# Row norms by halves of the columns, and part of the first block's softmax moved from VectorE to ScalarE, in a three-block transformer kernel

## The chip, the cores and the metric

The kernel runs on one core of one Trainium2 chip, as one launch. The metric is the device time of one execution in microseconds; lower is better. Engines are named as in the profile: PE is TensorE (PEld its weight loads), DVE is VectorE, ACT is ScalarE, POOL is GpSimd, SP is SyncE, which issues nearly all the DMAs.

## The reference, cut to what matters

Three transformer blocks are applied one after the other to one sequence of 256 rows of 1024 columns, all in fp32. Each block begins with a modulated RMS norm of the rows, and each ends with an RMS norm with a gain. In the first block the attention's softmax has one more logit per head, the sink:

```python
def rmsnorm(x, g):
    xf = x.astype(jnp.float32)
    y = xf * lax.rsqrt(jnp.mean(xf * xf, axis=-1, keepdims=True) + NORM_EPS)
    return (y * g.astype(jnp.float32)).astype(x.dtype)

# hybrid_layer, the first block
hx = modulate(rmsnorm(x, norm1_g), sh1x, sc1x)
hc = modulate(rmsnorm(ctx, norm1_g), sh1c, sc1c)
...
# windowed_attention: 16 heads, 256 own and 256 context keys
probs = jax.nn.softmax(jnp.concatenate([s_loc, s_ctx, sink_b], axis=-1), axis=-1)
p_loc = probs[..., :n_loc].astype(vn.dtype)
...
h2x = modulate(rmsnorm(x, norm2_g), sh2x, sc2x).reshape(B * L, D)
y = moe_ffn(h2x, w_router, b_router, w_gu, b_gu, w_down, b_down)
x = x + g2x * y.reshape(B, L, D)
```

## The kernel before

Rows lie on the 128 partitions, so the 256 rows are two tiles a = 0, 1 of 128 rows and 1024 columns. The stages run in this order, with their times in the profiled execution: the first block's projections, windowed attention, pooling and gates (0 to 318 us), its mixture of experts (318 to 1285), the second block's mixer (1285 to 1563), its peer layer (1563 to 2432), and the third block (2432 to the end at 2756). The expert weights stream through SP's DMA queue, and a loop at the end of that stage is a barrier for all engines.

Every fp32 weight tile is cut into two parts before PE uses it: ACT rounds it (`wh`, L151) and DVE subtracts (`wl`, L152); three matmuls per tile follow (L169, L194, L1707). Each of these helpers works tile by tile just ahead of PE, so a late `wl` or `wh` is a wait of PE.

The order on each engine is not the order of the code: a list scheduler places every instruction when the program is built, from its dependencies. A change of one stage therefore moves instructions of other work that lies beside it.

Norms: `rms_stats` (L310) takes for a = 0 the sum of squares on ACT (L318) and for a = 1 on DVE (L320), adds the constant on DVE (L321) and raises to the power -1/2 on POOL (L322). `scaled` (L325) multiplies the rows by it, a = 0 on DVE (L328) and a = 1 on ACT (L329). It is used by the first block for x and for the context, before the experts, and before the peer layer. `normed` (L332) joins the norm that ends a block with the norm that begins the next one (second and third block): two sums of squares per tile, L345 on ACT and L349 or L351, the product with the gain (L346), the power on POOL (L354) and the scaled rows (L355). `finish` (L358) later writes the rows of the residual stream. PE's transposes (L373) of the scaled rows follow, and `hl_T` writes their high and low parts (L414 to L422).

Attention of the first block: 16 turns (8 pairs of heads, two tiles of rows). `scores` makes for each of the two heads i the score matmuls on PE (L631, L632), bias and row minimum on DVE (L633, from PSUM), the exponentials on ACT (L635, with their sum), and the sink's share: a subtraction on DVE (L636) and a small exponential on ACT (L637). Then, one turn later, the sum and reciprocal on DVE (L647, L648), the normalization of both heads on DVE (L650, 128x512 each), the transposes on PE (L653) and the copies out of PSUM on ACT (L657) and DVE (L659). The modulation's weight sums (`ada_group`: ACT L291, DVE L292, POOL or DVE L294) are laid between the turns. Experts: the router's matmul is L832, its logits L834, its exponentials L845 on ACT, and the mask and ranks L850 to L880 on DVE.

Of the kernel before, what the change touches and what calls it, by code (L numbers as in the profile page):

```python
# [16 lines left out]
P = 128  # L17
# [4 lines left out]
D = 1024  # L22
# [6 lines left out]
def bcast_rows(ap1d, n=P):  # L29

    return ap1d.unsqueeze(0).broadcast_to([n, ap1d.shape[-1]])
# [28 lines left out]
def body(tc, A, out, stages=("b1", "moe", "b2", "peer", "b3"), dbg=None):  # L60
# [31 lines left out]
    with Pool("cst") as cst, Pool("ring", bufs=RING) as ring, Pool("psum", nb={"ps": 4, "pd": 3, "pa": 1}, space=PSUM) as psp:  # L92
# [217 lines left out]
        def rms_stats(pool, src, n, eps, tag="rs"):  # L310

            m = len(src)
            r = pool(tag + "_r", [P, m], bufs=2)
            for i, s in enumerate(src):
# [17 lines left out]
        def normed(pool, eps, tag, at_once=False):  # L332
# [6 lines left out]
            v = pool("nv", [P, 4])  # L339
            w = pool("nw", [P, 2])  # L340

            for a in range(2):
                v2, wa = v[:, 2 + a : 3 + a], w[:, a : a + 1]
                j = pool("b4", [P, D])
                nc.scalar.activation(j, x[:, a, :], AF.Square, accum_out=v[:, a : a + 1])  # L345
                nc.vector.tensor_tensor(xg[:, a, :], x[:, a, :], gb, ALU.mult)  # L346
                j = pool("b4", [P, D])
                if a == 0 and at_once:
                    nc.vector.tensor_tensor_reduce(j, xg[:, a, :], xg[:, a, :], 1.0, 0.0, ALU.mult, ALU.add, v2)  # L349
                else:  # L350
                    sq = nc.scalar.activation(j, xg[:, a, :], AF.Square, accum_out=v2)  # L351
                nc.vector.tensor_scalar(v2, v2, 1.0 / D, eps * eps1, ALU.mult, ALU.add)
                nc.vector.scalar_tensor_tensor(wa, v[:, a : a + 1], eps / D, v2, ALU.mult, ALU.add)
                nc.gpsimd.tensor_tensor(wa, wa, mhalf[:, 0:1], ALU.pow)  # L354
                ins = nc.vector.tensor_scalar(xs[:, a, :], xg[:, a, :], wa, None, ALU.mult)  # L355
            K.normed_by = (sq.ins, ins.ins)

            def finish():  # L358
                with K.tc.issue_after(K.parts_made.ins):
                    nc.vector.tensor_scalar(v[:, 0:2], v[:, 0:2], 1.0 / D, eps1, ALU.mult, ALU.add)  # L360
                nc.gpsimd.tensor_tensor(v[:, 0:2], v[:, 0:2], mhalf[:, 0:2], ALU.pow)
                nc.vector.tensor_scalar(x[:, 0, :], xg[:, 0, :], v[:, 0:1], None, ALU.mult)
                nc.scalar.activation(x[:, 1, :], xg[:, 1, :], AF.Copy, scale=v[:, 1:2])
# [164 lines left out]
def block1(K):  # L528
# [3 lines left out]
    with Pool("b1", nb=nb) as wp:  # L532
# [36 lines left out]
        nc.sync.dma_start(nsink, bcast_rows(A["attn_sink"]))  # L569
        nc.vector.tensor_scalar(nsink, nsink, -1.0, None, ALU.mult)  # L570
# [1549 lines left out]
```

## Time and profile before

| what | value |
|---|---|
| time, median of 3 runs | 2755.48 us (2755.38 to 2757.06) |
| the profiled execution | 2757.8 us |
| its span, first to last instruction | 2755.9 us |
| mean granted clock of TensorE | 0.974 of full speed |
| PE busy | 2572.7 us, 93% |
| DVE, ACT, POOL busy | 1532.8, 1022.6, 210.2 us |

The profiled execution lies 0.08% above the median, and 1.9 us of its time lie around its span. PE is the engine that is busy nearly always, so what matters is where PE waits, and for whom. An engine's busy share over the whole span says little: in the first block's attention DVE is at nine tenths in each slice of the page, in the experts' stage at one or two.

### The profile page before, as it was taken

To read this page: it belongs to the slowest core of one execution; us is meant where nothing else is said; L and a number is where in the kernel's file an instruction comes from. 1 tells how busy PE (TensorE), PEld (TensorE's weight loads), DVE (VectorE), ACT (ScalarE), POOL (GpSimd) and SP (SyncE) were. 2 spreads that over 40 slices of the span, in tenths; PEclk is the share of its full clock that TensorE was granted. 3 is DMA by queue.
4 is the path that set the end of the run, shared out by engine and by line. 5 is a ranking of instruction groups with operands and counts; after the bars stand their busy time and mean duration, and the time that the engine had idled before them with its cause. 6 is when DMAs were issued, how large, how long until landed. Compare 5 with 4: busy or idle time off the path is not lost. (4 is left out here: it accounts for less than half of the span.)

```text
span 2755.9 us, 36667 instructions
## 1 busy us (share of the span) xinstructions
PE 2572.7 (93%) x14235; PEld 1773.2 (64%) x14235; DVE 1532.8 (56%) x2574; ACT 1022.6 (37%) x1611; POOL 210.2 (8%) x125
## 2 busy tenths in 40 slices
PE   7999998999799979997999999999999999989998
PEld 4767742333233313333766798999888888878897
DVE  4997621122112201114787799687777675567777
ACT  3665300010001000002554443886555444455554
POOL 1221000000000000001112013100111000010000
PEclk9999999999999999999999999999999999999999
DMA  7668699999999999998565444679787785554452
GB/s 288 231 226 324 254 399 414 424 421 394 413 424 424 408 424 424 424 424 321 171 205 212 148 156 151 204 225 322 275 311 281 249 296 197 188 192 138 167 185 77
DMA packets 154017, 786.02 MB, mean 285 GB/s; under 512 B 14961, under 2 KB 49649, under 8 KB 70001
## 3 DMA queue, kind: packets, MB, share of 16 engines
q1 hardware_dynamic: 153840, 783.66, 75.0%
q8 instruction: 113, 1.85, 0.3%
q14 instruction: 64, 0.52, 0.0%
HBM read 765.78 MB, written 17.83 MB: 284 GB/s over the span
## 5 line engine op out<-in xcount | busy, mean ns | idle before, releaser
L152 DVE TENSOR_TENSOR wl<-w,wh 128x1024 fp32r<-128x1024 f32 x361 | 456.1, 1269 | 169.8 <-ACT wh L151 160.1
L151 ACT CAST wh<-w 128x1024 fp32r<-128x1024 f32 x379 | 393.1, 1042 | 341.1 <-PE pd L169 97.6
L169 PE MATMUL pd<-wh,b 128*128 128x512 f32 (+1 forms) x944 | 262.0, 395 | 1.1 <-POOL b L419 0.5
L936 PE MATMUL pd<-w,xd 128*64 128x512 f32 (+2 forms) x864 | 243.6, 606 | 3.9 <-DMA w<-in_w_gu 3.9
L169 PEld LDWEIGHTS pd<-wh,b 128*128 128x128 f32 x944 | 173.7, 189 | 46.4 <-issue 8.8
L1707 PE MATMUL pd<-wh,b 128*128 128x512 f32 x630 | 194.6, 390 | 1.3 <-DVE b L1692 0.7
L902 DVE TENSOR_SCALAR b<-pd 128x512 f32<-128x512 f32 x28 | 19.4, 691 | 254.1 <-PE pd L937 254.1
L169 PE MATMUL pd<-wl,b 128*128 128x512 f32 (+1 forms) x472 | 149.9, 396 | 5.9 <-DVE wl L152 5.9
L936 PEld LDWEIGHTS pd<-w,xd 128*64 128x64 f32 (+2 forms) x864 | 70.9, 133 | 114.2 <-issue 101.5
L955 DVE TENSOR_TENSOR b<-pd,g 128x512 f32<-128x512 f32 x28 | 19.3, 690 | 215.7 <-PE pd L937 215.7
L936 PE MATMUL pd<-wB,xd 128*64 128x512 f32 (+2 forms) x392 | 133.6, 601 | 4.9 <-DMA wB<-in_w_gu 4.9
L901 ACT ACTIVATE b<-b 128x512 f32<-128x512 f32 x28 | 17.7, 631 | 309.6 <-DVE b L900 309.6
L1707 PEld LDWEIGHTS pd<-wh,b 128*128 128x128 f32 x630 | 115.9, 188 | 24.0 <-DVE b L1692 1.1
L936 PE MATMUL pd<-w,at 128*64 128x512 f32 (+2 forms) x384 | 117.2, 667 | 13.1 <-DMA w<-in_w_down 12.5
L936 PE MATMUL pd<-wA,xd 128*64 128x512 f32 (+2 forms) x272 | 113.6, 646 | 4.8 <-DMA wA<-in_w_gu 4.8
L893 ACT ACTIVATE xd<-ps,mod,gs 128x128 f32<-128x128 f32 x56 | 25.2, 457 | 241.0 <-PE ps L889 162.4
L900 DVE TENSOR_SCALAR b<-pd 128x512 f32<-128x512 f32 x28 | 19.3, 690 | 165.0 <-PE pd L937 165.0
L1707 PE MATMUL pd<-wl,b 128*128 128x512 f32 x315 | 105.5, 389 | 0.0
L169 PEld LDWEIGHTS pd<-wl,b 128*128 128x128 f32 x472 | 87.3, 189 | 28.0 <-DVE wl L152 8.4
L1669 PE MATMUL ps<-b,wh 128*128 128x256 f32 x384 | 96.2, 292 | 2.8 <-ACT wh L151 2.8
L1575 DVE TENSOR_TENSOR b<-iota,slt 128x512 f32<-128x512 f32 x128 | 84.9, 711 | 21.1 <-PE pd L1583 21.1
L152 DVE TENSOR_TENSOR xT<-w,xT 128x1024 fp32r<-128x1024 f32 x53 | 67.1, 1266 | 50.6 <-ACT xT L151 50.6
(638 smaller groups left out, 5662.3 us busy)
## 6 DMA issues: line engine op xcount, KB each, us to landing
w<-in_w_gu SPq DMA_DIRECT2D x108, 1024.0 KB, 19.1
w<-in_peer_u SPq DMA_DIRECT2D x64, 1024.0 KB, 5.1
w<-in_peer_v SPq DMA_DIRECT2D x64, 1024.0 KB, 5.1
w<-in_w_down SPq DMA_DIRECT2D x59, 1024.0 KB, 19.5
w<-in_w_in SPq DMA_DIRECT2D x50, 1024.0 KB, 5.3
wB<-in_w_gu SPq DMA_DIRECT2D x49, 1024.0 KB, 19.6
w<-in_w_ada SPq DMA_DIRECT2D x48, 1024.0 KB, 6.4
wA<-in_w_gu SPq DMA_DIRECT2D x34, 1024.0 KB, 19.5
```

What stands on the lines that cost most here:

```text
L151: nc.scalar.copy(h, raw)
L152: (eng or nc.vector).tensor_tensor(l, raw, h.bitcast(F32), ALU.subtract)
L169: ins = mm(o, h[:, kk - k0 + k, a * P : (a + 1) * P], w[:, k * n : (k + 1) * n], start=(kk == k0 and m == 0 and k == 0), stop=(kk == k0 + ...
L893: nc.scalar.activation(d, s, AF.Identity, bias=sh[:, q : q + 1], scale=gs[:, q : q + 1])
L900: nc.vector.tensor_scalar(g, psg, 7.0, None, ALU.min)
L901: nc.scalar.activation(s, g, AF.Tanh, scale=0.851)
L902: nc.vector.tensor_scalar(l, psl, 7.0, -7.0, ALU.min, ALU.max)
L936: mm(ps[r], xt[:, k, r], ws[i][k // 4][:, k % 4, :], start=(k == 0), stop=False, skip_group_check=True)
L955: nc.vector.tensor_tensor(y, ps, g2[:, c * 512 : (c + 1) * 512], ALU.mult)
L1575: nc.vector.tensor_tensor(o, iota.unsqueeze(1).broadcast_to([P, 4, P]), SLT[:, v, t0 : t0 + 4].unsqueeze(2).broadcast_to([P, 4, P]), ALU.i ...
L1669: mm(o, wh[:, c], hh[:, k, :], start=(k == 0), stop=False)
L1707: ins = mm(acc[2 * a + c], p[:, i, a * P : (a + 1) * P], q[:, c * 512 : (c + 1) * 512], start=(first and i == 0 and n == 0), stop=(last an ...
```

## The change

Three edits are made. First, in `rms_stats` for rows of 1024 columns, and in `normed`, every square and every product with the gain is made for the left and the right 512 columns apart, with small additions that join the two sums; the scratch tiles come from the ring `b2` in place of `b4`. In `normed` the loop over the halves is the outer one and the loop over the tiles the inner one. Second, in `scores` the subtraction on DVE and the exponential over two columns are replaced by two exponentials over one column on ACT, with the sink as their bias; a copy of the sink row with its sign kept is made once on ACT. Third, the normalization of the second head of each turn (i = 1) is made on ACT with a scale in place of DVE.

```diff
@@ -311,6 +311,23 @@
 
             m = len(src)
             r = pool(tag + "_r", [P, m], bufs=2)
+            if n == D:
+
+                vs = [pool(tag + "_h", [P, 3], bufs=3) for _ in src]
+                for h in range(2):
+                    for i, s in enumerate(src):
+                        v, sh = vs[i], s[:, h * 512 : (h + 1) * 512]
+                        j = pool("b2", [P, 512])
+                        if i % 2 == 0:
+                            nc.scalar.activation(j, sh, AF.Square, accum_out=v[:, h : h + 1])
+                        else:
+                            nc.vector.tensor_tensor_reduce(j, sh, sh, 1.0, 0.0, ALU.mult, ALU.add, v[:, h : h + 1])
+                        if h == 0:
+                            nc.vector.tensor_scalar(v[:, 0:1], v[:, 0:1], n * eps, None, ALU.add)
+                        else:
+                            nc.vector.tensor_scalar(v[:, 2:3], v[:, 1:2], v[:, 0:1], 1.0 / n, ALU.add, ALU.mult)
+                            nc.gpsimd.tensor_tensor(r[:, i : i + 1], v[:, 2:3], mhalf[:, 0:1], ALU.pow)
+                return r
             for i, s in enumerate(src):
                 j = pool("b4", [P, n])
                 v = pool(tag + "_v", [P, 2], bufs=3)
@@ -336,31 +353,38 @@
             gb, eps1 = K.pending
             K.pending = None
             xg, xs = [pool(tag, [P, 2, D]) for _ in range(2)]
-            v = pool("nv", [P, 4])
-            w = pool("nw", [P, 2])
-
-            for a in range(2):
-                v2, wa = v[:, 2 + a : 3 + a], w[:, a : a + 1]
-                j = pool("b4", [P, D])
-                nc.scalar.activation(j, x[:, a, :], AF.Square, accum_out=v[:, a : a + 1])
-                nc.vector.tensor_tensor(xg[:, a, :], x[:, a, :], gb, ALU.mult)
-                j = pool("b4", [P, D])
-                if a == 0 and at_once:
-                    nc.vector.tensor_tensor_reduce(j, xg[:, a, :], xg[:, a, :], 1.0, 0.0, ALU.mult, ALU.add, v2)
-                else:
-                    sq = nc.scalar.activation(j, xg[:, a, :], AF.Square, accum_out=v2)
-                nc.vector.tensor_scalar(v2, v2, 1.0 / D, eps * eps1, ALU.mult, ALU.add)
-                nc.vector.scalar_tensor_tensor(wa, v[:, a : a + 1], eps / D, v2, ALU.mult, ALU.add)
-                nc.gpsimd.tensor_tensor(wa, wa, mhalf[:, 0:1], ALU.pow)
-                ins = nc.vector.tensor_scalar(xs[:, a, :], xg[:, a, :], wa, None, ALU.mult)
+            v = pool("nv", [P, 2, 2, 2])
+            w = pool("nw", [P, 2, 2])
+
+            for h in range(2):
+                c = slice(h * 512, (h + 1) * 512)
+                for a in range(2):
+                    va, wa = v[:, a], w[:, a, :]
+                    j = pool("b2", [P, 512])
+                    nc.scalar.activation(j, x[:, a, c], AF.Square, accum_out=va[:, 0, h : h + 1])
+                    nc.vector.tensor_tensor(xg[:, a, c], x[:, a, c], gb[:, c], ALU.mult)
+                    j = pool("b2", [P, 512])
+                    if a == 0 and h == 1 and at_once:
+                        nc.vector.tensor_tensor_reduce(j, xg[:, a, c], xg[:, a, c], 1.0, 0.0, ALU.mult, ALU.add, va[:, 1, h : h + 1])
+                    else:
+                        sq = nc.scalar.activation(j, xg[:, a, c], AF.Square, accum_out=va[:, 1, h : h + 1])
+                    if h == 0:
+                        nc.vector.tensor_scalar(wa[:, 1:2], va[:, 0, 0:1], eps, D * eps * eps1, ALU.mult, ALU.add)
+                        nc.vector.tensor_tensor(wa[:, 1:2], wa[:, 1:2], va[:, 1, 0:1], ALU.add)
+                        continue
+                    nc.vector.scalar_tensor_tensor(wa[:, 0:1], va[:, 0, 1:2], eps, va[:, 1, 1:2], ALU.mult, ALU.add)
+                    nc.vector.tensor_scalar(wa[:, 0:1], wa[:, 0:1], wa[:, 1:2], 1.0 / D, ALU.add, ALU.mult)
+                    nc.gpsimd.tensor_tensor(wa[:, 0:1], wa[:, 0:1], mhalf[:, 0:1], ALU.pow)
+                    ins = nc.vector.tensor_scalar(xs[:, a, :], xg[:, a, :], wa[:, 0:1], None, ALU.mult)
             K.normed_by = (sq.ins, ins.ins)
 
             def finish():
                 with K.tc.issue_after(K.parts_made.ins):
-                    nc.vector.tensor_scalar(v[:, 0:2], v[:, 0:2], 1.0 / D, eps1, ALU.mult, ALU.add)
-                nc.gpsimd.tensor_tensor(v[:, 0:2], v[:, 0:2], mhalf[:, 0:2], ALU.pow)
-                nc.vector.tensor_scalar(x[:, 0, :], xg[:, 0, :], v[:, 0:1], None, ALU.mult)
-                nc.scalar.activation(x[:, 1, :], xg[:, 1, :], AF.Copy, scale=v[:, 1:2])
+                    nc.vector.tensor_tensor(v[:, :, 0, 0], v[:, :, 0, 0], v[:, :, 0, 1], ALU.add)
+                    nc.vector.tensor_scalar(w[:, :, 1], v[:, :, 0, 0], 1.0 / D, eps1, ALU.mult, ALU.add)
+                nc.gpsimd.tensor_tensor(w[:, :, 1], w[:, :, 1], mhalf[:, 0:2], ALU.pow)
+                nc.vector.tensor_scalar(x[:, 0, :], xg[:, 0, :], w[:, 0, 1:2], None, ALU.mult)
+                nc.scalar.activation(x[:, 1, :], xg[:, 1, :], AF.Copy, scale=w[:, 1, 1:2])
 
             return xs, finish
 
@@ -567,6 +591,8 @@
         nc.gpsimd.memset(band[:, :, T : 2 * T], 0.0)
         nc.sync.dma_start(band[:, :, 0:T], A["c_band"])
         nc.sync.dma_start(nsink, bcast_rows(A["attn_sink"]))
+        sink = wp("sink", [P, 16])
+        nc.scalar.copy(sink, nsink)
         nc.vector.tensor_scalar(nsink, nsink, -1.0, None, ALU.mult)
 
         def bias(c):
@@ -633,8 +659,9 @@
                 nc.vector.tensor_tensor_reduce(p[:, i, :], ps, band[:, a, :], -1.0, nsink[:, h : h + 1], ALU.add, ALU.min, ng[:, i : i + 1])
             for i in range(2):
                 nc.scalar.activation(p[:, i, :], p[:, i, :], AF.Exp, scale=-1.0, bias=ng[:, i : i + 1], accum_out=es[:, 2 + i : 3 + i])
-            nc.vector.tensor_tensor(es[:, 0:2], ng, nsink[:, 2 * hp : 2 * hp + 2], ALU.subtract)
-            nc.scalar.activation(es[:, 0:2], es[:, 0:2], AF.Exp)
+            for i in range(2):
+                h = 2 * hp + i
+                nc.scalar.activation(es[:, i : i + 1], ng[:, i : i + 1], AF.Exp, bias=sink[:, h : h + 1])
             return p, es
 
         turns = [(hp, a) for hp in range(8) for a in range(2)]
@@ -647,7 +674,10 @@
             nc.vector.tensor_tensor(rs, es[:, 0:2], es[:, 2:4], ALU.add)
             nc.vector.reciprocal(rs, rs)
             for i in range(2):
-                nc.vector.tensor_scalar(p[:, i, :], p[:, i, :], rs[:, i : i + 1], None, ALU.mult)
+                if i == 0:
+                    nc.vector.tensor_scalar(p[:, i, :], p[:, i, :], rs[:, i : i + 1], None, ALU.mult)
+                else:
+                    nc.scalar.activation(p[:, i, :], p[:, i, :], AF.Copy, scale=rs[:, i : i + 1])
                 pt = pst()
                 for s in range(4):
                     nc.tensor.transpose(pt[:, s * P : (s + 1) * P], p[:, i, s * P : (s + 1) * P], ident)
```

In the whole program ACT has 1575 instructions in place of 1530 and DVE 2470 in place of 2472; PE, POOL and SP have the same numbers of instructions.

**DVE in a turn of the attention.** The tiles `b_269`, `b_280` are exponentials of two heads, `es` their sums, `rs` the reciprocals; L697 belongs to the pooling. Before:

```order
L668 TENSOR_TENSOR b_148_732<-pa_1216,b_147_731 128x256
L636 TENSOR_TENSOR es_1236<-ng_1235,nsink_111 128x2
L648 RECIPROCAL rs_287_1251<-rs_287_1251 128x2
L697 SCALAR_TENSOR_TENSOR b_385_1681<-pd_1706,cols_66,b_384_1680 128x256
L650 TENSOR_SCALAR b_269_1184<-b_269_1184,rs_287_1251 128x512 x2
L647 TENSOR_TENSOR rs_297_1290<-es_1236 128x2
L697 SCALAR_TENSOR_TENSOR b_385_1681<-pd_1715,cols_66,b_384_1680 128x256
L648 RECIPROCAL rs_297_1290<-rs_297_1290 128x2
L697 SCALAR_TENSOR_TENSOR b_385_1681<-pd_1724,cols_66,b_384_1680 128x256
L659 COPY b_286_1250<-ps_1262 128x4x128
L292 SCALAR_TENSOR_TENSOR aw_1180<-aw_1181,cpad_84,aw_1180 128x1024
```

And of the changed kernel, a turn further on (L674, L675 and L678 are the former L647, L648 and L650, L727 the former L697):

```order
L659 ISA b_297_1289,ng_1290<-ps_1296,band_116,nsink_117 128x512
L659 ISA ng_1290 128x1
L674 TENSOR_TENSOR rs_302_1304<-es_1250 128x2
L727 SCALAR_TENSOR_TENSOR b_390_1695<-pd_1720,cols_66,b_389_1694 128x256
L675 RECIPROCAL rs_302_1304<-rs_302_1304 128x2
L727 SCALAR_TENSOR_TENSOR b_390_1695<-pd_1729,cols_66,b_389_1694 128x256
L678 TENSOR_SCALAR b_285_1248<-b_285_1248,rs_302_1304 128x512
L292 SCALAR_TENSOR_TENSOR aw_1244<-aw_1245,cpad_84,aw_1244 128x1024
L674 TENSOR_TENSOR rs_318_1366<-es_1291 128x2
```

The subtraction into `es` is gone, and one multiplication stands where there were two. On ACT of the changed kernel the same turn reads as follows (L661 is the former L635, L664 the new sink exponential, L680 the new normalization, L687 the former L657):

```order
L726 ACTIVATE b_389_1694<-pd_1729,cols_66 128x256
L291 ACTIVATE aw_1244<-aw_1244,cpad_84 128x1024
L726 ACTIVATE b_389_1694<-pd_1738,cols_66 128x256
L661 ACTIVATE b_297_1289,es_1291<-b_297_1289,ng_1290 128x512
L664 ACTIVATE es_1291<-ng_1290,sink_455 128x1
L661 ACTIVATE b_297_1289,es_1291<-b_297_1289,ng_1290 128x512
L664 ACTIVATE es_1291<-ng_1290,sink_455 128x1
L680 ACTIVATE b_285_1248<-b_285_1248,rs_302_1304 128x512
L687 COPY b_290_1263<-ps_1308 128x4x128
```

The normalization of the tile `b_285` has come to stand behind the four exponentials of the next turn's tile `b_297`.

**ACT at the start of the experts' stage.** L318 is the sum of squares of tile 0, L393 the modulated transposes, L329 the scaled rows of tile 1, L845 the router's exponentials. Before:

```order
L318 ACTIVATE b_591_2690,rs_v_2691<-x_68 128x1024
L393 ACTIVATE wF_2623<-ps_2661,gs_2659 128x256
L393 ACTIVATE wF_2623<-ps_2668,gs_2659 128x256
L393 ACTIVATE wF_2623<-ps_2675,gs_2659 128x256
L393 ACTIVATE wF_2623<-ps_2682,gs_2659 128x256
L329 ACTIVATE b_578_2644<-x_68,rs_r_2689 128x1024
L845 ACTIVATE ex_2723,sm_2724<-tv_2715,ng_2721 128x4
L845 ACTIVATE ex_2752,sm_2753<-tv_2744,ng_2750 128x4
```

And of the changed kernel (L322, L417, L346 and L875 are the same steps):

```order
L322 ACTIVATE b_598_2706,rs_h_2704<-x_68 128x512
L417 ACTIVATE wF_2637<-ps_2675,gs_2673 128x256
L417 ACTIVATE wF_2637<-ps_2682,gs_2673 128x256
L417 ACTIVATE wF_2637<-ps_2689,gs_2673 128x256
L417 ACTIVATE wF_2637<-ps_2696,gs_2673 128x256
L322 ACTIVATE b_600_2712,rs_h_2704<-x_68 128x512
L346 ACTIVATE b_583_2658<-x_68,rs_r_2703 128x1024
L875 ACTIVATE ex_2743,sm_2744<-tv_2735,ng_2741 128x4
L875 ACTIVATE ex_2772,sm_2773<-tv_2764,ng_2770 128x4
```

The second half of the squares has come to stand behind the four modulated transposes.

**DVE in the second block's projections.** L152 makes the `wl` tiles, L1339 to L1341 (L1369 to L1371 in the changed kernel) a softmax over the forget-gate bounds with a 128x512 reciprocal, L1213 copies compressed keys out of PSUM. Before:

```order
L523 TENSOR_TENSOR b_1532_7175<-b_1560_7339,b_1561_7340 128x256 x2
L152 TENSOR_TENSOR wl_7386<-w_7349,wh_7385 128x1024
L152 TENSOR_TENSOR wl_7402<-w_7349,wh_7401 128x1024
L1339 TENSOR_TENSOR h_1699_7974<-lb_7442,lb_7443 128x512
L1340 RECIPROCAL h_1699_7974<-h_1699_7974 128x512
L511 TENSOR_TENSOR b_1574_7419<-b_1530_7173,rt_7096 128x512
L1341 TENSOR_TENSOR lb_7442<-lb_7442,h_1699_7974 128x512
L525 TENSOR_TENSOR b_1531_7174<-b_1574_7419,b_1575_7420 128x512
L511 TENSOR_TENSOR b_1576_7425<-b_1530_7173,rt_7096 128x512
L1213 COPY b_1599_7473<-ps_7474 64x255
L525 TENSOR_TENSOR b_1531_7174<-b_1576_7425,b_1577_7426 128x512
L1213 COPY b_1599_7473<-ps_7474 64x255
```

And of the changed kernel (L1195, L1197 and L1200 copy projections out of PSUM, L535 belongs to the rotation):

```order
L1369 TENSOR_TENSOR h_1710_8009<-lb_7477,lb_7478 128x512
L1197 COPY vs_7212<-pd_7214 128x128
L152 TENSOR_TENSOR wl_7311<-w_7288,wh_7310 128x560
L1195 COPY b_1544_7211<-pd_7215 128x256
L1370 RECIPROCAL h_1710_8009<-h_1710_8009 128x512
L1197 COPY vs_7212<-pd_7215 128x128
L152 TENSOR_TENSOR wl_7327<-w_7290,wh_7326 128x560
L152 TENSOR_TENSOR wl_7343<-w_7290,wh_7342 128x560
L1371 TENSOR_TENSOR lb_7477<-lb_7477,h_1710_8009 128x512
L152 TENSOR_TENSOR wl_7389<-w_7382,wh_7388 128x1024
L1200 COPY vs_7212<-pd_7292 128x128
L535 TENSOR_TENSOR b_1569_7366<-b_1541_7208,rt_7116 128x384
```

The reciprocal has moved up in front of the last two `wl` tiles of the 560-column projection; before, it stood behind all of these and ahead of the L1213 copies.

## Rows read from the trace of the kernel before

**Rows 1.** The page's busy times.

```profile
PE 2572.7 (93%) x14235; PEld 1773.2 (64%) x14235; DVE 1532.8 (56%) x2574; ACT 1022.6 (37%) x1611; POOL 210.2 (8%) x125
```

**Rows 2.** Stretches: length, busy us of five engines, granted clock, DMA; sum over 90 to 240.

```profile
110.00:120.00 10.00, 10.00 (x56) 7.87 (x55) 8.93 (x21) 5.80 (x15) 0.00 (x0) 0.89 0.78 261
...
sum 150.00, PE 137.82 PEld 100.13 DVE 133.03 ACT 90.08 POOL 26.75; mean PE 9.19 PEld 6.68 DVE 8.87 ACT 6.01 POOL 1.78
```

**Rows 3.** What PE waited for, 94 to 210: total, times, longest.

```profile
PE ps L653 <- DVE b L650: 4.6, 4, 2.7
...
PE ps L653 <- DVE es L636: 2.2, 1, 2.2
```

**Rows 4.** DVE groups, 94 to 206: busy us, mean ns, idle before.

```profile
L650 DVE TENSOR_SCALAR b<-b,rs 128x512 f32<-128x512 f32 x32 | 15.3, 512 | 0.2
...
L636 DVE TENSOR_TENSOR es<-ng,nsink 128x2 f32<-128x2 f32 x16 | 6.4, 401 | 0.0
```

**Rows 5.** Groups on ACT, 94 to 206.

```profile
L635 ACT ACTIVATE b<-b,ng 128x512 f32<-128x512 f32 x32 | 22.9, 716 | 7.4 <-DVE ng L633 7.3
...
L657 ACT COPY b<-ps 128x512 f32<-128x512 f32 x16 | 9.3, 579 | 9.7 <-PE ps L653 9.6
...
L637 ACT ACTIVATE es<-es 128x2 f32<-128x2 f32 x16 | 3.1, 194 | 2.5 <-DVE es L636 2.5
```

**Rows 6.** Timeline, 168 to 178.5: start, duration, instruction, [PE's idle time, who ended it].

```profile
168.63 2.35 POOL L294 TENSOR_TENSOR aacc<-aacc,aw 128x1024 f32<-128x1024 f32 x1 [18.94 <-DVE aw L292]
168.71 2.28 DVE L636 TENSOR_TENSOR es<-ng,nsink 128x2 f32<-128x2 f32 x1
...
171.38 0.87 DVE L650 TENSOR_SCALAR b<-b,rs 128x512 f32<-128x512 f32 x2
...
172.00 1.06 PE L653 MATMUL ps<-ident,b 128*128 128x128 f32 x8 [2.70 <-DVE b L650]
...
175.13 2.36 POOL L294 TENSOR_TENSOR aacc<-aacc,aw 128x1024 f32<-128x1024 f32 x1 [4.14 <-DVE aw L292]
...
176.24 1.53 DVE L650 TENSOR_SCALAR b<-b,rs 128x512 f32<-128x512 f32 x1
...
177.92 0.77 PE L653 MATMUL ps<-ident,b 128*128 128x128 f32 x5 [2.20 <-DVE es L636]
```

**Rows 7.** Timeline of PE, 106 to 112.

```profile
105.77 0.61 PE L169 MATMUL pd<-wh,b 128*128 128x512 f32 x2
108.93 1.22 PE L169 MATMUL pd<-wl,b 128*128 128x512 f32 x2 [2.55 <-DVE wl L152]
109.95 1.91 PE L653 MATMUL ps<-ident,b 128*128 128x128 f32 x8
```

**Rows 8.** Timeline of PE, 1322 to 1352.

```profile
1325.68 1.07 PE L169 MATMUL pd<-wh,b 128*128 128x512 f32 x4
...
1335.71 6.26 PE L1221 MATMUL ps<-w,b 128*32 128x128 f32 x32 [3.98 <-DVE b L1218]
...
1346.90 3.65 PE L1221 MATMUL ps<-w,b 128*32 128x128 f32 x32 [0.47 <-issue]
```

**Rows 9.** Timeline of DVE, 1322 to 1343.

```profile
1325.68 3.35 DVE L1340 RECIPROCAL h<-h 128x512 f32<-128x512 f32 x1
```

**Rows 10.** Timeline of ACT, 318 to 328.

```profile
319.77 1.55 ACT L393 ACTIVATE wF<-ps,gs 128x256 f32<-128x256 f32 x4
321.82 1.15 ACT L329 ACTIVATE b<-x,rs_r 128x1024 f32<-128x1024 f32 x1 [0.49 <-POOL rs_r L322]
323.77 0.30 ACT L845 ACTIVATE ex<-tv,ng 128x4 f32<-128x4 f32 x1 [0.81 <-DVE ng L842]
```

**Rows 11.** Timeline of DVE, 318 to 328.

```profile
321.84 0.74 DVE L328 TENSOR_SCALAR b<-x,rs_r 128x1024 f32<-128x1024 f32 x1
```

**Rows 12.** Timeline of POOL, 316 to 328.

```profile
320.71 1.07 POOL L322 TENSOR_TENSOR rs_r<-rs_v,mhalf 128x1 f32<-128x1 f32 x2
```

**Rows 13.** The squares of L318 by forms: shortest, median, longest ns.

```profile
L318 ACT ACTIVATE b<-b x2: 628/844/1061, 17.6 to 2516.9; 128x1024 f32<-128x1024 f32 x1, 128x512 f32<-128x512 f32 x1
```

## The prediction

> **What bounds the kernel now.** I read the page's busy times first: PE works in 93% of the span [rows 1], so a change of other engines' work can only shorten PE's waits or lengthen them. Which waits the edits can touch is a question of place, so I next read busy times by stretches. In the attention, between 90 and 240 us, PE is busy for 137.8 of 150 us, DVE for 133.0 and ACT for 90.1 [rows 2]: 12.2 us of PE's time are idle there, with DVE nearly full and ACT at six tenths. The list of PE's waits says who ended them: 4.6 us in four waits end with a normalization L650 and 2.2 us in one with the subtraction L636, all in front of the transposes L653 [rows 3]. These are the two operations that the change takes off DVE, 6.8 us of waits in all.
>
> The groups give the prices. A normalization takes 512 ns in the mean, the subtraction 401 ns for two columns [rows 4], which is far too long for its size. The timeline shows why: at 168.71 the subtraction lasts 2.28 us and ends with POOL's addition L294, which began at 168.63 and lasts 2.35; at 176.24 a normalization lasts 1.53 us beside POOL's next addition, while two of them took 0.87 us together at 171.38 when POOL was idle [rows 6]. PE's two longest waits for these operations, 2.70 us ahead of 172.00 and 2.20 us ahead of 177.92, come directly behind these held operations [rows 6].
>
> A wait can also cost afterwards. Behind an idle time of 2.55 us at 108.93 (it ended with a `wl` of DVE) two matmuls take 1.22 us that took 0.61 before it, and eight transposes 1.91 us [rows 7] where eight take 1.06 [rows 6]; the stretch 110 to 120 has a granted clock of 0.89 [rows 2]. TensorE went from its 2.4 GHz level to 1.2 GHz after that idle time. I price it at 0.6 + 0.9 + 0.3 for the matmul behind them = 1.8 us. The two waits of rows 6 have normal durations behind them.
>
> **The change part by part.**
>
> *Attention.* DVE loses sixteen normalizations at 0.435 us (half of 0.87) = 7.0 us, and sixteen subtractions, 6.4 us as they stand [rows 4]; without the held one of 2.28 us [rows 6] the other fifteen take 4.1, and a second one may be held too, so 2 to 4 us of it are the operations' own. ACT gains sixteen normalizations. Its nearest rows for 128x512 are the copy out of PSUM at 579 ns and the exponential at 716 ns [rows 5]; I take 0.63, 10.1 us. The sink exponentials become 32 in place of 16 at 194 ns [rows 5], +3.1 us at most. So ACT goes from 6.0 to at most 6.9 tenths, while DVE falls from 8.9 to between 8.0 and 8.2 (133.0 less 10 to 13.4, of 150). ACT's idle time there ends mostly with something that PE (9.6 us ahead of L657) or DVE (7.3 us ahead of L635) made [rows 5], so ACT has room, though not necessarily at the right moment: in the new order a normalization stands behind the four exponentials of the next turn. The sink's chain also loses a hop from DVE to ACT, for which ACT waited 2.5 us [rows 5].
>
> What can PE get back? At most all of its idle time, 12.2, and the 1.8 us of clock: 14 us. At least nothing, if the waits only move. The named waits and the clock loss make 6.8 + 1.8 = 8.6 us. SP's loads are reordered too, but no wait of rows 3 ends with a DMA, so I cost that at nothing; a late weight tile would show as a wait for `wh` on ACT. I choose two thirds of the 8.6, 6 us, since the order leaves half of the normalizations, all of the `wl` subtractions and POOL's additions where they can meet, and the transposes of the second head now wait for ACT.
>
> *Norms of whole rows.* A square of 512 columns on ACT takes 628 ns against 1,061 for 1024 [rows 13]: two halves are 0.2 us longer than one whole, and one small addition more lies in the chain. At the start (x, context) and ahead of the peer layer PE waits for this chain with nothing else to do: +0.3 us at each of these two places (bounds 0, where a half can begin before the rest of the rows is there, and 0.5). In the third block's `normed`, ACT has seven halves at 0.63 us = 4.4 us where it had three wholes at 1.06 = 3.2 us, and both tiles' second halves come behind all first halves: between 0 and +1.2; I take +0.4, as the transposes of tile 1 hide part. In the second block I take 0 for the norm itself (bounds -0.5 and +0.5).
>
> *Start of the experts' stage.* Here the order matters. ACT's first half ends 0.4 us earlier than the whole did, so the four L393 (1.55 us, until now from 319.77 [rows 10]) run from about 319.4 to 320.95; the second half, 0.63, and the read of its sum end at about 321.7. One addition and a power on POOL (half of 1.07 us [rows 12]) later, at 322.5, DVE can scale tile 0, for 0.74 us, where it did so at 321.84 [rows 11]. Tile 1's last addition stands behind that on DVE; its power ends at about 324.1, and ACT's scaling of tile 1 (1.15 us) at 325.2. The router's exponential is queued behind it and began at 323.77 [rows 10]: +1.4 us. Everything on DVE behind the exponential (mask, ranks) shifts with it, and the experts' stream of weights starts when the first blocks are made. Bounds: 0, if other work hides it, and 1.9.
>
> *Second block.* The scheduler moves the 3.35 us reciprocal [rows 9]. It stood ahead of the copies and additions that L1221 waits for; PE idles 3.98 us there and the 32 matmuls take 6.26 us, against 3.65 us when they run a second time [rows 8], 2.6 us of lowered clock. With the reciprocal earlier this goes, -6.6 us. In its new place it delays two `wl` tiles; of its 3.35 us PE's matmuls on the tile before cover 1.07 [rows 8] and the two low ones 0.6 [rows 7], leaving 1.7 us. Two copies out of PSUM now stand ahead of a `wl` there (about 0.5 each by the 579 ns for 512 columns [rows 5]), 1.0 us, and `finish` takes its power on POOL later, half of 1.07 [rows 12], 0.6 us. Net -3.3 us; bounds -6.6 (no new wait) and +3.3 (the new ones come and the old one stays).
>
> **Sum.** -6 - 3.3 + 0.3 + 0.3 + 0.4 + 1.4 = -6.9 us. Against the profiled execution's 2757.8 us this is 2750.9; that execution is 2.3 us above the median of 2755.48, so for the median I predict 2748.6 us. Within 0.2%, 5.5 us, a measurement of this kernel hardly tells a change from none, and my forecast lies just beyond this.
>
> **A rule beside the rows.** The Trainium skill (SBUF — State Buffer, Who interferes with whom) says that VectorE and GpSimd share a port pair, that an operation with two SBUF inputs or in a mode that uses both ports waits out a GpSimd operation that reads SBUF, and that ScalarE waits on nobody. Rows 6 agree: the subtraction and the multiplication were held, and the waits ended with POOL. By that rule the sixteen operations on ACT can't be held any more, but POOL's additions stay, and hold whatever comes next on DVE; that is rival 1.
>
> **Rivals.**
>
> 1. *The holds and queues only move.* POOL's additions last as long as before, and DVE's next operation from SBUF (the sum L647, the remaining normalization, a `wl`) is held in place of L636. The 2.70 and 2.20 us waits then stay. For it: DVE remains above eight tenths. Against it: 10 us less work on DVE must let its queue catch up. With 2 us from the attention, half of the second block's gain and the losses of 2.4: 2755.5 - 2 - 1.6 + 2.4 = 2754.3.
>
> 2. *ACT is late (slower).* The normalization is queued behind exponentials and a 1.15 us L291 on ACT, and the transposes of the second head wait. Nothing is won from the attention then, and each microsecond by which the sixteen are late is PE's. With 3.3 won and 2.4 lost elsewhere, the kernel is slower by over 5.5 us from 0.4 us a turn on (16 x 0.4 = 6.4); one L291's worth, 0.7 us beyond the slack, gives 11.2 - 0.9: 2765.8. Against it stand the idle times of rows 5. The Trainium skill (ScalarE: Activation LUTs, Rules for kernel authors) advises multiplications on VectorE rather than ScalarE; the rows bear out only that one is dearer on ACT (0.58 to 0.72 against 0.435 us).
>
> 3. *All of DVE's waits go.* -14 in the attention, -3.3, +2.4: 2740.6 us.
>
> 4. *The second block's stall stays and the new ones come*: 6.6 us worse than my sum, 2755.2; this merges with rival 1.
>
> **How the numbers follow.** I give my forecast 0.45 (its own range 2744 to 2753), rivals 1 and 4 together 0.29, rival 2 0.14 and rival 3 0.12. The forecast's case reaches "faster" in six of seven cases, rival 3 always: 0.38 + 0.12 = 0.50. Within 0.2%: 0.07 of the forecast, rivals 1 and 4, and a mild rival 2: 0.38. Slower: 0.12. The range 2742 to 2758 leaves out most of rival 3 and the worse part of rival 2, under 2 in 10.
>
> **What will show it.** Right: the waits for L650 and L636 in front of L653 fall from 6.8 us to about 2, no wait of over 1 us for ACT's normalization appears, and 110 to 120 us has a full clock; the router's exponential comes later by 1.4 us relative to the end of the residual; L1221's first 32 matmuls take under 4.5 us. The prediction is wrong if PE waits for ACT at L653 in each turn, if DVE's waits stay with other names, or if the second block has both stalls.

## The result, and the profile after

The changed kernel takes 2768.34 us (median of 5 runs, 2765.73 to 2775.85) against 2755.48: a ratio of 1.0059 with an interval of 1.0046 to 1.0072. It is slower by 13 us where I had forecast 7 us faster. In a later set of runs the same kernel gave 1.0059 again (1.0038 to 1.0081). Its profiled span is 2766.6 us, 10.7 more than before; single executions of one kernel differ by several microseconds, in their stages too. First and last starts of some lines show where the difference arises:

| point in the program | before, us | after, us | difference |
|---|---|---|---|
| last residual row of the first block (DVE L436) | 317.9 | 319.2 | +1.4 |
| first expert matmul (PE L936) | 335.5 | 342.9 | +7.4 |
| last expert matmul | 1279.9 | 1287.6 | +7.7 |
| peer layer, first matmul of its up projection (L1669) | 1632.6 | 1636.0 | +3.4 |
| peer layer, first matmul of its down projection (L1707) | 1899.6 | 1900.7 | +1.1 |
| its last one | 2431.7 | 2440.7 | +9.0 |
| span | 2755.9 | 2766.6 | +10.7 |

Two stages lose most, the experts' start and the peer layer's down projection, and in this pair of executions the second block gains back some. At the experts' start the page of busy times shows nothing, but PE's timeline of the changed kernel does (start, duration, instruction, idle time before and who ended it; L862 is the router's matmul, the former L832):

```profile
329.48 2.90 PE L862 MATMUL ps<-wr,wF 128*128 128x128 f32 x12 [8.63 <-DMA wr<-in_w_router]
```

PE waits 8.63 us for the load of the router's weights. Why is it late? SP issues it, and SP's timeline shows what stands ahead:

```profile
285.99 32.38 SPq L807 DMA_DIRECT2D wA<-in_w_gu  x2
...
319.41 0.65 SPq L844 DMA_DIRECT2D wr<-in_w_router  x1
```

The two early expert loads `wA` take 32.38 us to issue: the first goes out at 285.99, the second only at 318.04, and the router's load, behind them on the same queue, at 319.41. In the kernel before, SP issued both `wA` within 0.91 us and the router's load at 291.31:

```profile
284.62 0.91 SPq L777 DMA_DIRECT2D wA<-in_w_gu  x2
...
291.31 0.57 SPq L814 DMA_DIRECT2D wr<-in_w_router  x1
```

What `wA` waits for stands in SP's list of waits (280 to 325 us):

```profile
SPq L807 <- PE pd L169: 21.0, 2, 20.6
SPq L807 <- DVE b L431: 11.0, 1, 11.0
```

These are readers and writers of tiles of the first block. `wA` has no use of their data; it needs their place in SBUF. The halved norms take their scratch tiles from the ring `b2` in place of `b4`. I take it that a pool lays its rings out in the order of their first use; the runs with padding below bear this out. Then in the first block the large ring `b8` begins 8192 bytes lower than before (four tiles of 2048 bytes ahead of it in place of four of 4096), and a place that the experts' stage wants early is now held by the next tile of that ring. That this tile is in use for longer is my reading of the two waits; no run moves `b8` by padding alone.

The second loss is of another kind: PE is busy throughout. Four matmuls in a row of the peer layer's down projection, first in the changed kernel (L1737), then in that of before:

```profile
2303.14 1.10 PE L1737 MATMUL pd<-wh,b 128*128 128x512 f32 x4
```

```profile
2301.36 1.07 PE L1707 MATMUL pd<-wh,b 128*128 128x512 f32 x4
```

The last of the four takes 0.39 us, so the other three follow each other every (1.07 - 0.39) / 3 = 0.227 us before and every 0.237 after, at a granted clock of 1.00 in both. Averaged over the 1500 or so matmuls of that line that follow another without idle time, from start to start, it is 0.227 before and 0.234 after; the spacings below are this average where no stretch is named. On the line's 1536 matmuls 0.007 us each are 11 us; from its first to its last matmul the stage takes 532.1 us before and 540.0 after.

The attention answers [rows 3, 5] as follows (PE's waits from 94 to 210; groups of ACT and DVE from 94 to 206; L680 is the moved normalization, L664 the sink exponential, L674 the former L647; L722 is a matmul of the pooling):

```profile
PE pd L722 <- DVE b L727: 3.6, 1, 3.6
...
PE ps L683 <- DVE rs L674: 1.6, 1, 1.6
PE ps L683 <- DVE rs L675: 1.0, 1, 1.0
PE ps L683 <- DVE b L678: 1.0, 2, 0.8
```

```profile
L680 ACT ACTIVATE b<-b,rs 128x512 f32<-128x512 f32 x16 | 11.3, 716 | 0.5 <-DVE rs L675 0.5
...
L664 ACT ACTIVATE es<-ng,sink 128x1 f32<-128x1 f32 x32 | 8.3, 281 | 0.0
```

The waits for the normalization and the subtraction, 6.8 us [rows 3], seem to have become 1.0, but that takes the names too literally. The transposes L683 do not read `rs`; at both waits put down to `rs` a normalization L678 had ended 0.07 or 0.08 us earlier, at 149.47 and 195.95. So 3.6 us in front of the transposes are still DVE's, and behind held operations as before:

```profile
146.81 1.94 DVE L674 TENSOR_TENSOR rs<-es 128x2 f32<-128x2 f32 x1
193.87 2.08 DVE L678 TENSOR_SCALAR b<-b,rs 128x512 f32<-128x512 f32 x1
```

Both lie beside an addition L294 on POOL (146.36 to 148.73 and 193.27 to 195.67); L674 takes 0.15 us at 149.38. The sixteen normalizations left on DVE take 693 ns in the mean in place of 512, while ACT's sixteen lie between 706 and 727 ns and none is held. To this comes a new wait of 3.6 us. DVE, POOL and PE around it:

```profile
172.85 0.67 DVE L674 TENSOR_TENSOR rs<-es 128x2 f32<-128x2 f32 x1
173.44 0.47 DVE L727 SCALAR_TENSOR_TENSOR b<-pd,cols,b 128x256 fp32r<-128x256 f32 x1
```

```profile
171.14 2.36 POOL L294 TENSOR_TENSOR aacc<-aacc,aw 128x1024 f32<-128x1024 f32 x1 [2.90 <-DVE aw L292]
```

```profile
173.97 1.22 PE L722 MATMUL pd<-b,w 128*128 128x256 f32 x2 [3.57 <-DVE b L727]
174.98 1.99 PE L683 MATMUL ps<-ident,b 128*128 128x128 f32 x8
```

POOL's addition ends at 173.50; the two-column sum L674 takes 0.67 us and ends with it, and L727 and PE come behind. The hold is some 0.5 us of the 3.57; for the rest L727, whose input from ACT was ready at 170.88, stood in DVE's queue behind a copy and two row minima (170.91 to 172.9). PE's eight transposes then take 1.99 us against 1.06 [rows 6]: TensorE has fallen to its 1.2 GHz level, and the granted clock of 170 to 180 us is 0.66 where it was 1.00 before. It is my rival 1, in three places, and in this one with the clock loss that the two long waits of [rows 6] did not have. PE's idle time between 90 and 240 us is 12.0 us; it was 12.2.

### The profile page after: what moved, and what is told of

Its sections match the earlier page's. It is cut to its first block, busy times and chain, and to the rows that moved or that the text cites. A ratio compares the mean times of both kernels' runs of the same rounds, so it can differ in the third digit from the quotient of the medians.

```text
span 2766.6 us, 36769 instructions
## 1 busy us (share of the span) xinstructions
PE 2577.8 (93%) x14235; PEld 1770.8 (64%) x14235; DVE 1531.8 (55%) x2572; ACT 1038.2 (38%) x1668; POOL 213.2 (8%) x125
## 5 line engine op out<-in xcount | busy, mean ns | idle before, releaser
L152 DVE TENSOR_TENSOR wl<-w,wh 128x1024 fp32r<-128x1024 f32 x361 | 459.8, 1279 | 180.1 <-ACT wh L151 170.7
L1737 PE MATMUL pd<-wh,b 128*128 128x512 f32 x630 | 198.4, 396 | 0.0
L1737 PEld LDWEIGHTS pd<-wh,b 128*128 128x128 f32 x630 | 116.2, 188 | 26.1 <-DVE b L1722 0.3
L1737 PE MATMUL pd<-wl,b 128*128 128x512 f32 x315 | 107.9, 397 | 0.0
L152 DVE TENSOR_TENSOR xT<-w,xT 128x1024 fp32r<-128x1024 f32 x53 | 67.1, 1266 | 54.5 <-ACT xT L151 54.5
```

What stands on the lines that cost most here:

```text
L152: (eng or nc.vector).tensor_tensor(l, raw, h.bitcast(F32), ALU.subtract)
L1737: ins = mm(acc[2 * a + c], p[:, i, a * P : (a + 1) * P], q[:, c * 512 : (c + 1) * 512], start=(first and i == 0 and n == 0), stop=(last an ...
```

## The experiments

All ratios are to the kernel before, run on the same chip in the same set.

| run | ratio, interval | first block's last row, us | PE's wait for the router's load | down projection of the peer layer, us |
|---|---|---|---|---|
| before | 1 | 317.9 | none | 532.1 |
| after | 1.0059, 1.0046 to 1.0072 | 319.2 | 8.6 | 540.0 |
| e1_soft | 0.9995, 0.9979 to 1.0011 | 311.4 | none | 533.2 |
| e2_norm | 1.0057, 1.0036 to 1.0079 | 316.0 | 8.4 | 540.8 |
| e3_b4 | 1.0015, 1.0002 to 1.0028 | 316.5 | none | 534.2 |
| f1_b4_first | 1.0045, 1.0031 to 1.0059 | 318.0 | none | 542.9 |
| f2_b4_peer | 1.0047, 1.0033 to 1.0060 | 319.3 | 8.6 | 531.1 |
| h1_mix | 0.9982, 0.9969 to 0.9995 | 314.6 | none | 529.7 |

**Which edit?** One run has the softmax edits alone, one the norms by halves alone.

> Kernel before with the softmax edits alone (sink exponentials and every second normalization on ScalarE), norms as before. Theory A (the loss comes from the norms' edit: with the scratch tiles in the ring b2 the tiles of the first block lie elsewhere, the weight load wA waits for late readers of its place, and the router's load behind it on SP's queue comes 28 us later): no wait of PE for the router's load, and the experts' first matmul at 335.5 give or take 2 us; time 2751 to 2757. Rival B (the softmax edits themselves cost, by a normalization that ACT makes late): experts' first matmul 4 to 8 us later than before, time 2760 to 2765.

> The changed kernel with the softmax edits undone, so the norms by halves alone. Theory A: PE waits 7 to 10 us for the router's load at the start of the experts, the experts' first matmul is at 342 to 345, time 2762 to 2768. Rival B: no such wait, time 2752 to 2758.

The norms by halves alone carry the whole loss (2770.1 us, above theory A's range, with the experts' first matmul at 340.7, before its range), and the softmax edits alone none (2752.3). In the first run's profile the experts begin at 330.2, earlier than either theory had it, and the first block ends 6.5 us earlier; the time does not show it, so I ran it again later (below).

**The scratch ring.** The changed kernel again, with one line in `rms_stats` and the same twice in `normed`:

```diff
-                        j = pool("b2", [P, 512])
+                        j = pool("b4", [P, D])[:, 0:512]
```

> The changed kernel with one difference: the scratch tiles of the halved squares come from the ring b4 again, as in the kernel before. Theory A: the place of the first block's tiles is as before, SP issues wA before 290 us, PE's wait for the router's load (8.6 us) is gone and the experts begin 7 to 9 us earlier than in the changed kernel; time 2756 to 2762. A rival by which the halves themselves make the experts' start late (ScalarE's second half behind the four transposes): the experts still begin at 341 to 343, time 2766 to 2769.

Of the 0.59% of loss 0.44 go with the scratch ring, some 12 us, while every square is still halved. SP issues `wA` at 283.25 in 0.90 us, and the wait of 8.6 us is gone. A control, the changed kernel again beside these:

> The changed kernel again, as a control on the same chip. In its profile the 128x512 matmuls follow each other every 0.234 us from 1880 us on, in that of the kernel before every 0.227 us until 2480, which is 8 us over the peer stage. If that belongs to the kernel, it is there again in every profile of it, and time is 2766 to 2772; if it belongs to the single execution, the spacing is 0.227 in some profile of this kernel and the time can be 8 us lower.

It gave 2772.61 us, and its matmul spacing was 0.234 again, while e1_soft and e3_b4 had 0.227 and e2_norm 0.234. So the spacing belongs to the kernel, and it too follows the ring. Are these two effects? The next two runs use the old ring in some stages only, by the constant `eps` that tells the stages apart:

```diff
-                        j = pool("b2", [P, 512])
+                        j = pool("b4", [P, D])[:, 0:512] if eps == 1e-5 else pool("b2", [P, 512])
```

> The changed kernel with the scratch tiles of the norms back in the ring b4 in the first block and the experts' stage alone; the peer layer keeps b2. If two separate effects of the place of tiles add up to the loss (late loads at the experts' start, and 3% longer spacing of the matmuls in the peer layer): PE's wait for the router's load is gone, the experts begin 7 to 9 us earlier than in the changed kernel, the spacing from 1900 us on stays 0.234, and the time is 2760 to 2765. If the spacing follows from something in the first block: it is 0.227 here.

> The mirror of this: b4 in the peer layer alone, b2 in the first block and the experts. Two separate effects: PE still waits 8 to 9 us for the router's load, the spacing in the peer layer is 0.227 to 0.229, and the time is 2760 to 2765. If the spacing has another cause than the place of the peer's tiles: 0.234.

In the profiles both came out as two separate effects would: the one has no wait for the router and the slow spacing, the other the wait of 8.6 us and 0.227. The times are 2763.53 and 2765.62 us, the second just above its range. Each takes back 0.12 to 0.14% in the timed ratio, 3 to 4 us, with intervals that overlap that of the changed kernel. That e3_b4 takes back 12 is more than their sum. But e3_b4 also moves the scratch of `normed`, in the second and third block, which neither of these two does; what that is worth was not measured, so 4 to 5 of the 12 us stay without a cause of their own.

**Queue or place?** In the changed kernel the router's load stands behind `wA`, but its own place might be taken as well. Here the loads of the router, `iota` and `tri` are moved ahead of the five early expert loads.

> The changed kernel with the loads of the router, the iota and the triangle issued ahead of the five early expert loads. If only the queue makes the router's load late (it stands behind wA on SP): it is issued at about 286 us and PE's wait of 8.6 us is gone. If its own place is taken too until the last rows of the first block are written (its wait for DVE): it is issued at 315 to 320 all the same, and PE's wait stays at 7 to 9 us.

Neither was right. SP's timeline of this run:

```profile
311.58 0.57 SPq L842 DMA_DIRECT2D wr<-in_w_router  x1
...
313.37 3.98 SPq L807 DMA_DIRECT2D wA<-in_w_gu  x2
```

The load's own place is free at 311.58, late but early enough: PE's wait is gone and the experts begin at 334.9. The experts still end 3.8 us later than before (1283.7); a single timing gave 2772.72. From first to last matmul the experts take 948.8 us here, and 942.9 to 945.7 in every other profile. Late loads of their weights are the likely reason, since the DMA share is 1.01 in most of that stage before and after (424 GB/s), but no run isolates it. So the queue made the router late, and by this one execution the late places cost about half of the 7.7 us by themselves.

**Is it the place that makes the spacing?** First two shifts of the kernel before, with no other change than the padding of the peer layer's pool, 104 words, made 1128 and 107.

> The kernel before with nothing changed but the place of the peer layer's tiles: 4096 bytes more padding per partition ahead of them, which is the distance by which the other scratch ring moves them in the changed kernel. If the place alone makes the matmuls' spacing: 0.233 to 0.236 us from 1900 to 2430 us in place of 0.227, and the time 6 to 9 us above before. If it needs the changed instructions: 0.227, time as before within 3 us.

> The kernel before with 12 bytes more padding per partition at the same place, which is what the longer statistics tiles of the halved norms add. If the small shift matters (the versions with halved norms and the old ring had 0.228 to 0.229): spacing 0.228 to 0.230 and time 1 to 3 us above before; if not: 0.227 and the time of before.

The first gave 0.9996 (0.9982 to 1.0009) and 0.227: shifting all later tiles together does nothing. The second gave 1.0002 (0.9988 to 1.0016); its spacing is 0.230 until 2240 us and 0.227 from there, so the shift shows in the spacing and not in the time. In these matmuls the weights come from the ring `b2` and the streamed tiles mostly from `wh` and `wl`. By the sizes of the tiles, `b2` and `wh` agree modulo 2048 bytes in the kernel before and in all versions so far with fast spacing, while they are 608 bytes apart in the changed kernel. Four more runs tested this relative place, with padding alone:

```diff
 k1, changed kernel, peer layer
-        wp("pad", [P, 104])
+        wp("pad", [P, 256])
 k2 and k3, kernel before, peer layer, ahead of the ring b2 (152 or 64 words)
+                wp("padz", [P, 152])
 k4, version h1, third block, ahead of the ring f2
+            wp("padf", [P, 240])
```

> The changed kernel with 608 bytes more padding per partition between the ring b2 and the later tiles of the peer layer, so that b2 and wh agree modulo 2048 again. If the relative place of weights and streamed tiles makes the spacing: 0.227 to 0.230 us in the peer layer and 6 to 9 us less than the changed kernel, 2760 to 2766. If it is the region in which b2 lies (low, beside xT) or anything else in the change: 0.234 to 0.236 still, 2768 to 2772.

> The kernel before with 608 bytes of padding ahead of the ring b2 in the peer layer, all instructions the same. If the relative place makes it: spacing 0.234 to 0.236 and 6 to 9 us more than before, 2759 to 2762. If not: 0.227 and the time of before.

> The same with 256 bytes. The first two blocks have offsets that are multiples of 256 bytes and a spacing of 0.228 to 0.230. If only the offset modulo 256 counts: 0.227 and the time of before. If weights and streamed tiles must agree modulo 2048: 0.234, 6 to 9 us more.

> The version from the parts (h1) with 960 bytes of padding ahead of the ring f2 in the third block, whose tiles are the weights of its down projection; the offset to wh, 1088 bytes, becomes 0. If the relative place makes the spacing there too: the 264 matmuls of 128x512 from 2500 us on follow each other every 0.227 in place of 0.235 us, 2 us less than h1 (2746). If not: 0.235 and the time of h1.

Groups of the down projection from 2260 to 2400 us, of k1 (L1737) and of k2 (L1708):

```profile
L1737 PE MATMUL ps<-wh,b 128*128 128x512 f32 x66 | 25.7, 389 | 0.0
```

```profile
L1708 PE MATMUL ps<-wh,b 128*128 128x512 f32 x66 | 26.2, 396 | 0.0
```

And the third block's down projection from 2500 to 2740 us, of h1 (L1947) and of k4 (L1948):

```profile
L1947 PE MATMUL ps<-wh,f 128*128 128x512 f32 x44 | 17.4, 395 | 0.0
```

```profile
L1948 PE MATMUL ps<-wh,f 128*128 128x512 f32 x44 | 17.1, 389 | 0.0
```

The spacing was 0.227 in k1, 0.234 in k2, 0.227 in k3, and in k4's third block 0.227 from 2600 us on, where the kernel before and h1_mix have 0.234 to 0.235. Padding alone takes the changed kernel's slow spacing away and gives it to the kernel before. k3 also shows that the two rings need not agree modulo 2048: 256 bytes apart are as good.

The times follow less well: k1 1.0044 (1.0028 to 1.0060), k2 1.0014 (1.0002 to 1.0027), k3 0.9997 (0.9987 to 1.0008), k4 0.9988 (0.9974 to 1.0003). k1's median of 2768.16 us lies above its range of 2760 to 2766, its ratio is only 0.15% under that of the changed kernel, and the intervals overlap; k4 is not faster than h1_mix. k2's time rises by 4 us by the ratio (5 by the medians) of the 6 to 9 expected, though its down projection takes 543.6 us, 11.5 more than before's. Over all profiles that projection takes 528.5 to 536.1 us in the versions with the fast spacing and 540.0 to 543.6 in those with the slow one. Why less of this arrives in the median stays open, so the size of this effect is less certain than its cause.

**A version from the parts.** Softmax edits, halves only in `normed`, with scratch in `b4`, and whole-row statistics in the other four places.

> A version from the parts: softmax edits, norms by halves only where two norms are joined (second and third block) with scratch in b4, and whole-row norms as before at the other four places. The places of the tiles in the first block, the experts and the peer layer are those of the kernel before. If the halves of the first block, the experts and the peer layer bring nothing by themselves and the joined ones gain in the second block: 2746 to 2752. If the joined halves bring nothing either: as with the softmax edits alone, 2749 to 2755.

It is the first that beats the kernel before: 0.9982, and in a second set, where the softmax edits alone ran beside it, 0.9976 (0.9962 to 0.9990) against 0.9990 (0.9977 to 1.0002).

> The version from the parts again, beside the softmax edits alone on the same chip. If the joined norms by halves gain by themselves (the second block's wait for L1221 becomes 2.6 in place of 4.0 us, at full clock behind it), this one is 1 to 4 us below the other; if not, both agree within 1 us.

> The softmax edits alone again. In its first profile the first block ended 6 us earlier than in the kernel before, while the timed runs gave a ratio of 0.9995. If the timed ratio is the truth: 0.998 to 1.001 again, and the first block's end in this profile differs from 311 us; if the profile is: a ratio of 0.9975 to 0.999.

The joined norms' gain over the softmax edits alone, 2748.6 and 2747.7 us against 2752.3 and 2753.1, is 4 to 5 us by the medians, just under 4 by the ratios, with intervals that overlap. The softmax edits alone are worth between nothing and 3 us: their second profile has the first block's end at 314.5.

## Why the prediction was wrong

**The step that failed** is the sentence "SP's loads are reordered too, but no wait of rows 3 ends with a DMA, so I cost that at nothing". Rows 3 covers 94 to 210 us, and the wait came at 320.9, ahead of the experts. I looked at what waits had ended with before, not at what the loads would wait for after. The change names the ring of the scratch tiles, and I never asked what the ring's new place does to others: neither to loads into a place that comes free later, nor to the matmuls of a stage 1300 us behind. None of my rivals had this mechanism. It was worth 8.6 us of wait at the experts' start (7.7 at their end) and 8 us in the peer layer's down projection; my sum had 1.4 at the first of these places and no term at the second. That `b8` would move could be worked out from the sizes of the tiles without a run; that `wA` would then wait for PE (21.0 us) and DVE (11.0) I know from the trace alone. Rival 2's 2765.8 us lies near the measured time, but by luck: what it describes did not happen.

**Attention**, forecast -6: the first block ends 1.4 us later. Of the 6.8 us of named waits 3.6 stayed under other names, which I had given as a sign of being wrong, and a new one of 3.6 came, with the lower clock behind it. That is rival 1, to which I had given less than my forecast. Two of my signs were right: 110 to 120 us has a granted clock of 1.00, and no wait of PE in that list ends with ACT, so rival 2 is out. ACT's share came out as reckoned (6.9 tenths from 90 to 240 us), DVE's fell only to 8.5 in place of 8.0 to 8.2. A normalization costs 716 ns on ACT, not the 0.63 us that I took, and a sink exponential 281 ns for one column, more than the 194 ns for two. Without the halved norms of the first block the same softmax edits start its last residual row at 310.9 to 314.6 us (five profiles: e1_soft, h1_mix, each twice, and k4), where the instructions of the kernel before start it at 316.2 to 317.9 (five) and the changed kernel's own at 317.2 to 319.3 (five, with e4_wr). So a gain of the forecast's kind was possible, about 4 us in the mean, but not in this order of the program.

**Start of the experts**, forecast +1.4 for ACT's order: right, and hidden behind the larger wait. In f1_b4_first, which has the same instructions without that wait, the router's exponential begins at 325.41, 7.4 us behind the start of the last residual row at 318.01; before it was 5.9 (323.77 less 317.87). My walk had ACT's scaling end at 325.2; there it ends at 325.50.

**Second block**, forecast -3.3: the peer layer's first up matmul is 4.3 us nearer to the experts' end. L1221 (now L1251) answers to [rows 8]:

```profile
1345.38 3.68 PE L1251 MATMUL ps<-w,b 128*32 128x128 f32 x32 [2.60 <-DVE b L1248]
```

The wait shrank from 3.98 to 2.60 us in place of going, and the clock behind it stayed up: 3.68 us in place of 6.26. This part holds in every profile: the wait is 2.6 us in all eleven versions with joined halves and 4.0 in all seven without, and the first 32 matmuls take 3.68 us in eight of the eleven (5.3 in three), 5.2 to 6.5 in the seven. The net gain is another matter. From the last expert matmul to the first up matmul the profile before takes 352.7 us, but four other executions of the same instructions 349.1 to 350.7; the changed kernel takes 348.4 and, in its control, 351.9. Most of the 4.3 us is thus the luck of one profile, and a net gain of the size forecast is not shown for the changed kernel.

**Whole-row halves**, forecast +0.3, +0.3 and +0.4: at the first block's start PE's first transposes come 0.16 us later (9.85 for 9.69); ahead of the peer layer PE waits 4.78 us against 4.42; in the third block 6.20 and 0.63 us against 3.16 and 0.90. From the end of the last residual row, 2434.4 and 2443.4, to the first transposes it is 4.3 and 5.9 us: +1.6, above my upper bound of 1.2, as both tiles' second halves wait for all first halves.

## What to carry to other kernels

A change of scratch tiles is a change of the memory map. Before costing instructions, ask whose place each early load takes in the new layout and what it will wait for there; a load that waits holds up every load behind it on its queue. And when the same matmuls are slower at a full granted clock, look at where their two operands lie to each other.

## What the runs showed of the hardware that I had not expected

The pace of a 128x512 matmul depended on where its weights lay relative to the streamed tile, at the same granted clock: 0.227 us each with offsets of 0 and 256 bytes modulo 2048 between the two rings, 0.234 with 608 bytes (peer layer), 0.234 to 0.235 with 1088 bytes (third block). The offsets are worked out from the sizes of the tiles in the kernel's text, and they are those of whole tiles: in the peer layer the weights of one matmul are 512 bytes within such a tile, beginning at 0, 512, 1024 or 1536. The granted clock was 1.00 from 2280 to 2420 us in the kernel before, the changed one, k1, k2 and k3. Padding alone switched the pace both ways in the peer layer and from slow to fast in the third block. Which offsets in between are slow, and what in the memory makes it, was not tried. A shift of all later tiles together by 12 bytes of padding gave 0.230 in the first part of the down projection only, which this does not explain.
